# Two layer entries of a hybrid decoder step: zero products at the start, weights and squares queued elsewhere

## The chip, the core and the metric

The kernel runs on one core of a Trainium2 chip. The engines are named as in the profile: PE (TensorE; PEld is its weight load), DVE (VectorE), ACT (ScalarE), POOL (GpSimd) and SP (SyncE, which here only issues DMAs). Each takes its instructions in the order in which they were laid out. The metric is the device time of one execution in microseconds; a kernel's time is the median of its runs.

## The reference, cut to what matters

One inference step of two layers over 1024 prompt tokens and 8 x 8 sample tokens, 1088 rows of 1024 in all. Layer 0 is a Mamba-2 SSD mixer, layer 1 latent attention (MLA). The change touches how each layer begins:

```python
ln_p = rms_norm(hp, norm_w[i]); ln_s = rms_norm(hs, norm_w[i])
# layer 0
proj = jnp.einsum('btd,de->bte', h, w_in)           # 1024 -> 2048 + 4096 + 32
xbc, new_buf = causal_conv(xbc, conv_buf, conv_w, conv_b)   # needs the last 3 rows of state_conv
# layer 1
proj = jnp.einsum('btd,de->bte', h, w_in)           # 512 + 256 + 32 + 1024 (gate)
```

`rms_norm` divides each row by the root of its mean square and multiplies with a weight per column. Everything is float32.

## The kernel before, in words

Each operand of a large product is held as two float32r parts, high and low: `split` (L123) casts on ACT and subtracts on DVE or POOL. A product is then three matmuls, high-high, high-low, low-high (`proj_piece`, L84 inside `mm3`).

The rows are handled as nine tiles (`TILES`: eight of 128, one of 64) in three token groups (`TG`: 384, 384, 320). `norm_steps` is the entry of both layers. For each group, `norm_cols` takes eight column steps `d`: three transposes on PE into a PSUM tile `xtp` (L244), the high part on ACT with the norm weight as scale (L246, tile `xh` in the first layer, `hh` in the second; the instructions are kept in `k.cols`), and the low part on DVE (L247, `xl`, `hl`). Between column steps, `steps` runs one piece of projection per group and block.

First entry (`norm_rows`): rows are loaded by SP (L704, L706; `XB` buffers), squared on ACT with a running sum (L227), and the inverse root is taken by DVE (L198) and POOL's power (L203), for the first group row by row, for the other two once a group; DVE scales the row (L234). The squares of the next group are queued on ACT behind column step `SQ + j` of the group before. The function `before` loads the small vectors and the weights of projection blocks 0 and 1, each in two parts (`WPARTS`, L281, cast L125, low part L126). The function `after` runs behind the first group: `ssd_consts` (small constants, `alog`, masks) and `conv_state_T`, which loads 96 state rows (`cst`, L316) and transposes them on PE (`cvp`, L321). Block 2's weights are cast behind the eighth column of the first group; their DMAs are not held. Their low parts and those of the gate weights `zd` (`load_zdt`, L337 to L341) are made on POOL. Blocks 0 and 1 are projected together, group by group, then blocks 2 and 3, then the gates (`pz`, L96).

Second entry (`tail=True`): the rows `xrb` come out of the last projection of the SSD layer (`ssd_out`; DVE adds L804, L806), are stored to `h_d`, squared on ACT into a spare tile `tok` (L814), and scaled by `scale_row` (L209). The rows 6 to 8 are scaled ahead of the first column step. Two gate blocks (`gate_block`: weights `wgh`, `wgl`, the low part on POOL) are projected together meanwhile; the evacuation of their pieces is a SiLU on ACT (L921).

Who goes first on an engine is decided by a planner that lays all instructions out on a modelled clock. `issue_after(ins)` adds an edge: what is traced inside it on the engine of `ins` is laid out behind `ins`, without a wait for its end. `keep_in_program_order` puts one instruction behind everything traced before it on its engine.

Of the kernel before, what the change touches and what calls it, by code (L numbers as in the profile page):

```python
# [16 lines left out]
D = 1024  # L17
# [41 lines left out]
XDB = 2  # L59
SQ = 2  # L60
YB = 2
SCAN = "csccsccsccscc"
XB = 6
WPARTS = 2
# [57 lines left out]

def split(k, hi, lo, src, eng=None):  # L123
    nc = k.nc
    nc.scalar.copy(hi, src)  # L125
    (eng or nc.vector).tensor_tensor(lo, src, hi.bitcast(F32), op=ALU.subtract)  # L126
# [69 lines left out]
def rstd_of(k, out, ssq, n):  # L196
    nc = k.nc
    nc.vector.tensor_scalar(out, ssq, 1.0 / n, EPS, op0=ALU.mult, op1=ALU.add)  # L198
    m, n = out.shape[0], int(np.prod(out.shape[1:]))
    e = k.nhalf[:m, :n]  # L200
    if len(out.shape) == 3:
        e = e.rearrange("p (a b) -> p a b", a=out.shape[1])
    nc.gpsimd.tensor_tensor(out, out, e, op=ALU.pow)  # L203

# [8 lines left out]
def norm_rows(k, gi, load, pool, xbufs):  # L213
# [7 lines left out]
    for j, i in enumerate(idx):  # L221
# [3 lines left out]
        sq = k.sqp(f"sq{i}")  # L225
        with k.tc.issue_after(k.cols[gi - 1][SQ + j].ins) if gi else nullcontext():
            nc.scalar.activation(sq[:m], xt[:m], AF.Square, accum_out=ssq[:m, j : j + 1])  # L227
# [10 lines left out]
def norm_cols(k, gi, xs, wcol, hi, lo, psum):  # L238
    nc = k.nc
    t0, n = TG[gi]  # L240
    for d in range(8):
        p = psum.tile([128, 512], F32, tag="tr", name=f"xtp{gi}_{d}", bufs=PB["tr"])
        for xt, m, o in xs:
            nc.tensor.transpose(p[:, o : o + m], xt[:m, d * 128 : d * 128 + 128], k.ident[:m, :m])  # L244
        k.cols[gi].append(
            nc.scalar.activation(hi[:, d, t0 : t0 + n], p[:, :n], AF.Copy, scale=wcol[:, d : d + 1]))  # L246
        nc.vector.scalar_tensor_tensor(  # L247
            lo[:, d, t0 : t0 + n], p[:, :n], wcol[:, d : d + 1], hi[:, d, t0 : t0 + n].bitcast(F32),
            op0=ALU.mult, op1=ALU.subtract)
    if gi == 2:  # L250
# [3 lines left out]
def norm_steps(k, load, wcol, hi, lo, pool, psum, steps, xbufs, before=None, after=None, tail=False):  # L254
    if tail:
        for i in range(6, 9):
            k.hrows.append(scale_row(k, i, pool))
    rows = k.hrows[:3] if tail else norm_rows(k, 0, load, pool, xbufs)
    if before is not None:
        before()  # L260
        wcol = k.normc[0]
    k.cols = [[], [], []]
# [15 lines left out]

def load_w(k, pool, src, nk, ncol, tag, bufs=3, raws=None, rbufs=2, eng=None):
# [4 lines left out]
    split(k, hi, lo, raw, eng)  # L284
    return hi, lo


def load_parts(k, pool, src, nk, parts, tag, bufs, raws=None, rbufs=2, eng=None):
    n = nk // parts
    return [x for j in range(parts)  # L290
            for x in kslices(load_w(k, pool, src[128 * n * j : 128 * n * j + 128 * n], n, src.shape[1], tag, bufs,
                                    raws, rbufs, eng), n)]

# [124 lines left out]
class Group:  # L418
# [28 lines left out]

    def weights(self, bi):
        k, g = self.k, self.g
        col = (DIN + DIN + 128 * g, DIN + DIN + 1024 + 128 * g, DIN + 256 * g, DIN + 256 * g + 128)[bi]  # L450
        return load_parts(k, self.wp, k.I["ssd_w_in"][0][:, col : col + 128], 8, WPARTS, "wi", WB, self.raws.get(bi), RB,
                          k.nc.gpsimd if g == 0 and bi > 1 else None)
# [246 lines left out]
def x_loader(k):  # L699
    I = k.I  # L700

    def load(xt, i):
        if i < 8:
            k.nc.sync.dma_start(xt, I["x_prompt"][0, i * 128 : i * 128 + 128])  # L704
        else:
            k.nc.sync.dma_start(xt[:64], I["x_sample"].rearrange("b t d -> (b t) d"))  # L706

# [81 lines left out]
def ssd_out(k, items, ypools, psum):  # L789
# [3 lines left out]
    for n, (ph, i) in enumerate(items):  # L793
# [3 lines left out]
        for hf in range(2):  # L797
# [13 lines left out]
        (nc.gpsimd if ph.k0 and i > 6 else nc.sync).dma_start(k.h_d[t0 : t0 + m], xr[:m])  # L811
        if ph.k0:
            sq = k.tok.rearrange("p i a h -> p (i a h)")[:, :D]
            nc.scalar.activation(sq[:m], xr[:m], AF.Square, accum_out=k.hssq[:m, i : i + 1])  # L814
            rstd_of(k, k.hrs[:m, i : i + 1], k.hssq[:m, i : i + 1], D)
            k.hr.append((xr, m))
            if i < 6:
                k.hrows.append(scale_row(k, i, k.h0p))
# [3 lines left out]
def layer_ssd(k):  # L822
# [8 lines left out]
    with ExitStack() as st:  # L831
# [14 lines left out]
        with open_pool(tc, name="x0", bufs=1, side="right") as p0:  # L846
# [15 lines left out]
        for _ in range(6):  # L862
            next(st0)
# [52 lines left out]
def gate_block(k, wp, raws, b):  # L916
    ws = kslices(load_w(k, wp, k.I["mla_w_in"][0][:, 800 + 128 * b : 928 + 128 * b], 8, 128, "wg", 3, raws, eng=k.nc.gpsimd), 8)
    gt = wp.tile([128, T], F32, tag="gt", name=f"gt{b}", bufs=2)
# [1073 lines left out]
```

## Time and profile before

| | |
|---|---|
| median of three runs | 1969.62 us |
| runs | 1965.58, 1969.62, 1971.59 us |
| profiled execution, its own time | 1968.92 us |
| its span in the profile | 1967.1 us |
| mean granted clock of PE | 0.992 |
| DMA over the span | 202.00 MB, mean 103 GB/s |

The span runs from the first to the last instruction of the profiled execution; the time of an execution has a little more around it. A row of the timeline reads: start, duration (of all that is merged in the row), engine, line, operation, output tile, input tiles, shapes, count, and in brackets how long the engine had idled and what ended it. `x2` behind a row means that two instructions are merged into it. Matmul durations overlap, so their starts give the rate. In the waits, the numbers are the total in us, the count and the longest.

### The profile page before, as it was taken

The page shows a single profiled execution, that of the slowest core. Times are in us where ns is not written, and L with a number is a line of the kernel's source. Part 1 is how long each engine was busy: PE and PEld are TensorE (multiplying, and loading weights), DVE is VectorE, ACT ScalarE, POOL GpSimd, SP SyncE. Part 2 cuts the span into 40 slices and gives each one's busy share as a digit, 9 for nine tenths or more (in the row PEclk, how much of TensorE's full clock was granted, in tenths as well). Part 3 has the DMA queues.
Part 4 walks back from the last instruction along what each step waited for, and adds up shares of the span by engine and source line. Part 5 has one row for each costly group of instructions (what it writes and reads, how often), then busy time and mean ns, then how long its engine had stood idle before and what let it go on. Part 6 is the DMA issues. An engine that isn't in the chain of part 4 may idle for free. (4 is left out here: it accounts for less than half of the span.)

```text
span 1967.1 us, 33409 instructions
## 1 busy us (share of the span) xinstructions
PE 1902.0 (97%) x12001; PEld 1732.5 (88%) x12001; DVE 1188.6 (60%) x2407; ACT 1109.2 (56%) x2535; POOL 822.2 (42%) x1017
## 2 busy tenths in 40 slices
PE   6999999999999999899999999999999999899998
PEld 5999999999999999788787998898888888688887
DVE  4547566666665666765533104466787887666674
ACT  5456666666666676742214314335777776755552
POOL 1537555555655555444003212103343434745441
PEclk9999999999999999999999999999999999999999
DMA  5223333333333332554534333132121113554441
GB/s 153 59 59 89 95 85 94 85 103 88 92 86 94 78 101 68 194 169 148 183 116 116 121 146 95 56 107 76 46 68 40 51 42 86 180 188 143 143 126 38
DMA packets 181085, 202.00 MB, mean 103 GB/s; under 512 B 18828, under 2 KB 147608, under 8 KB 180536
## 3 DMA queue, kind: packets, MB, share of 16 engines
q1 hardware_dynamic: 175864, 180.08, 30.1%
q0 software_dynamic: 4976, 19.66, 3.0%
q8 instruction: 95, 1.56, 0.3%
q14 instruction: 70, 0.57, 0.1%
q10 hardware_dynamic: 80, 0.13, 0.0%
HBM read 146.52 MB, written 53.28 MB: 102 GB/s over the span
## 5 line engine op out<-in xcount | busy, mean ns | idle before, releaser
L84 PE MATMUL pj<-xh,wih 128*128 128x384 f32 (+1 forms) x768 | 255.3, 336 | 4.4 <-ACT xh L246 3.9
L84 PE MATMUL pj<-xl,wih 128*128 128x384 f32 (+1 forms) x768 | 254.8, 332 | 0.6 <-DVE xl L247 0.6
L84 PE MATMUL pj<-xh,wil 128*128 128x384 f32 (+1 forms) x768 | 254.1, 331 | 0.0
L1354 POOL TENSOR_TENSOR tl<-P,th 128x384 fp32r<-128x384 f32 (+1 forms) x96 | 90.7, 945 | 238.5 <-ACT P L1352 192.7
L483 DVE SCALAR_TENSOR_TENSOR acc<-raw,vec,acc 128x1112 f32<-128x1112 f32 x96 | 142.1, 1481 | 25.7 <-ACT acc L479 24.7
L84 PEld LDWEIGHTS pj<-xh,wih 128*128 128x128 f32 x768 | 144.6, 189 | 6.3 <-ACT xh L246 4.5
L84 PEld LDWEIGHTS pj<-xl,wih 128*128 128x128 f32 x768 | 145.1, 189 | 1.9 <-DVE xl L247 0.9
L84 PEld LDWEIGHTS pj<-xh,wil 128*128 128x128 f32 x768 | 145.0, 189 | 0.4
L96 PE MATMUL pz<-wih,xh 128*128 128x256 f32 x504 | 142.8, 287 | 1.1 <-ACT z L524 1.1
L96 PE MATMUL pz<-wil,xh 128*128 128x256 f32 (+1 forms) x504 | 140.2, 284 | 0.0
L1351 ACT ACTIVATE th<-st 128x512 fp32r<-128x512 f32 x192 | 94.4, 492 | 73.0 <-PE st L1347 52.6
L587 ACT ACTIVATE M<-M,tok 128x128 f32<-128x128 f32 (+1 forms) x288 | 90.9, 386 | 68.2 <-DVE M L584 67.9
L96 PE MATMUL pz<-wih,xl 128*128 128x256 f32 x448 | 128.3, 286 | 0.0
L1639 POOL TENSOR_TENSOR kvl<-pgr,kvh 128x512 fp32r<-128x512 f32 x64 | 85.3, 1350 | 74.3 <-ACT kvh L1637 74.3
L96 PEld LDWEIGHTS pz<-wih,xh 128*128 128x128 f32 x504 | 95.9, 190 | 1.9 <-ACT z L524 1.6
L584 DVE TENSOR_TENSOR M<-M,negu 128x512 f32<-128x512 f32 x64 | 52.2, 816 | 69.8 <-DMA M<-acs_d 69.6
L1352 ACT ACTIVATE P<-st 128x512 f32<-128x512 f32 x192 | 93.5, 487 | 0.0
L96 PEld LDWEIGHTS pz<-wil,xh 128*128 128x128 f32 (+1 forms) x504 | 92.7, 184 | 0.7
L126 DVE TENSOR_TENSOR wil<-wraw,wih 128x512 fp32r<-128x512 f32 x88 | 70.5, 807 | 29.5 <-ACT wih L125 26.6
L96 PEld LDWEIGHTS pz<-wih,xl 128*128 128x128 f32 x448 | 85.3, 190 | 0.1
L570 POOL TENSOR_TENSOR xdd<-xsT,tok 128x256 f32<-128x256 f32 x64 | 50.8, 794 | 80.4 <-ACT xsT L556 80.0
L1354 DVE TENSOR_TENSOR tl<-P,th 128x512 fp32r<-128x512 f32 x96 | 69.2, 721 | 21.9 <-ACT P L1352 21.5
(826 smaller groups left out, 6296.3 us busy)
## 6 DMA issues: line engine op xcount, KB each, us to landing
wraw<-in_ssd_w_in SPq DMA_DIRECT2D x92, 256.0 KB
M<-acs_d SPq DMA_DIRECT2D x64, 256.0 KB
s<-in_state_ssm SPq DMA_DIRECT2D x32, 256.0 KB
y_d<-y SPq DMA_DIRECT2D x64, 128.0 KB
out_s_ssm<-s SPq DMA_DIRECT2D x32, 256.0 KB
wraw<-in_ssd_w_out SPq DMA_DIRECT2D x12, 512.0 KB
q_d<-qt SPq DMA_DIRECT2D x32, 192.0 KB
qp<-q_d SPq DMA_DIRECT2D x8, 768.0 KB
```

What stands on the lines that cost most here:

```text
L84: nc.tensor.matmul(out, a, b, start=(i == 0), stop=(i == n - 1))
L96: nc.tensor.matmul(o, a, b, start=(j == 0), stop=(j == len(ops) - 1))
L126: (eng or nc.vector).tensor_tensor(lo, src, hi.bitcast(F32), op=ALU.subtract)
L483: last = nc.vector.scalar_tensor_tensor(acc, raw[:, j : j + n], k.convw[j][:, blk : blk + 1], acc, op0=ALU.mult, op1=ALU.add)
L570: nc.gpsimd.tensor_tensor(v3(xdd), v3(xsT), hb(2), op=ALU.mult)
L584: nc.vector.tensor_tensor(M[:m, :, :m], M[:m, :, :m], (k.negs if smp else k.negu)[:m, :m].unsqueeze(1).to_broadcast([m, 4, m]), op=ALU.add)
L587: nc.scalar.activation(M[:m, h, :m], M[:m, h, :m], AF.Exp, bias=tk[:, 0, 4 * g + h : 4 * g + h + 1])
L1351: nc.scalar.activation(th[:, :n], ps[:, :n], AF.Exp, scale=SCALE)
L1352: nc.scalar.activation(P[:, :n], ps[:, :n], AF.Exp, scale=SCALE)
L1354: eng.tensor_tensor(tl[:, :n], P[:, :n], th[:, :n].bitcast(F32), op=ALU.subtract)
L1639: nc.gpsimd.tensor_tensor(rl[:, j : j + 2], raw[:, j : j + 2], rh[:, j : j + 2].bitcast(F32), op=ALU.subtract)
```

## The change

1. An activation table is loaded at the start of ACT's queue.
2. Eight products of a zeroed tile (128x128 by 128x256, plain float32) are put at the start, two more behind the second and one behind the third transpose of column step 1 of the first group. Nothing reads their output.
3. The cast and subtraction of the second part of block 1's weights are queued behind the third column step (`late`).
4. In the first entry each row gets its own inverse root, the squares of the next group come one column step later, and there is one row buffer more.
5. `conv_state_T` runs behind the second group; `ssd_consts` is traced behind the whole entry, its exponential and masks held behind late instructions of the entry.
6. Block 2's weights are loaded behind the last x row on SP and cast behind the eighth column of the second group.
7. In the second entry the last row is squared behind the third column step, the last three rows are scaled behind low columns 4 to 6 (counted from 0), and the store of the last row is issued behind the first group.
8. The low part of the gate weights is made in four instructions instead of one.

```diff
-SQ = 2
+WARM = (8, 2, 1)
+SQ = (3, 3)
-XB = 6
+XB = 7
@@ split: parts > 0 subtracts in that many slices
+    for a in range(parts):
+        s = slice(a * n, a * n + n)
+        (eng or nc.vector).tensor_tensor(lo[:, s], src[:, s], hi[:, s].bitcast(F32), op=ALU.subtract)
@@ setup
+    tc.keep_in_program_order(nc.scalar.preload_act_table_set("exp_and_others"))
@@ ssd_consts
-    nc.scalar.activation(k.alog, k.alog, AF.Exp)
+    with k.tc.issue_after(k.cols[1][7].ins):
+        nc.scalar.activation(k.alog, k.alog, AF.Exp)
...
-        nc.gpsimd.tensor_scalar(neg, mask, -NEG, NEG, op0=ALU.mult, op1=ALU.add)
+        with k.tc.issue_after(k.pow.ins):
+            nc.gpsimd.tensor_scalar(neg, mask, -NEG, NEG, op0=ALU.mult, op1=ALU.add)
@@ new
+def warm_open(k, pool, psum):
+    k.wsrc = pool.tile([128, 256], F32, name="wsrc")
+    k.nc.gpsimd.memset(k.wsrc, 0.0)
+    k.wout = psum.tile([128, 512], F32, tag="pj", name="wout", bufs=PB["pj"])
+
+def warm(k, n):
+    for _ in range(n):
+        k.nc.tensor.matmul(k.wout[:, :256], k.wsrc[:, :128], k.wsrc, start=True, stop=True)
+
+def square_row(k, i, junk):
+    xr, m = k.hr[i]
+    k.nc.scalar.activation(junk[:m], xr[:m], AF.Square, accum_out=k.hssq[:m, i : i + 1])
+    rstd_of(k, k.hrs[:m, i : i + 1], k.hssq[:m, i : i + 1], D)
@@ norm_rows
-        with k.tc.issue_after(k.cols[gi - 1][SQ + j].ins) if gi else nullcontext():
+        with k.tc.issue_after(k.cols[gi - 1][SQ[gi - 1] + j].ins) if gi else nullcontext():
...
-        if gi == 0:
-            rstd_of(k, rs[:, j : j + 1], ssq[:, j : j + 1], D)
-    if gi:
-        rstd_of(k, rs, ssq, D)
+        k.pow = rstd_of(k, rs[:, j : j + 1], ssq[:, j : j + 1], D)
@@ norm_cols
+            if k.late and d == 1 and j:
+                with k.tc.issue_after(tr.ins):
+                    warm(k, WARM[j])
...
+        if d == 2 and k.late:
+            with k.tc.issue_after(k.cols[gi][-1].ins), k.tc.issue_after(k.lows[-1].ins):
+                split(k, *k.late.pop())
@@ norm_steps
-    if tail:
-        for i in range(6, 9):
-            k.hrows.append(scale_row(k, i, pool))
...
+        if tail and gi == 0:
+            with k.tc.issue_after(k.cols[0][2].ins), k.tc.issue_after(k.lows[2].ins):
+                square_row(k, 8, pool.tile([128, D], F32, tag="sq", name="hsq8", bufs=1))
+            for i in range(6, 9):
+                with k.tc.issue_after(k.lows[i - 2].ins):
+                    k.hrows.append(scale_row(k, i, pool))
...
-        if after is not None and gi == 0:
+        if after is not None and gi == 1:
             after()
...
+        if tail and gi == 0:
+            xr, m = k.hr[8]
+            k.tc.keep_in_program_order(k.nc.gpsimd.dma_start(k.h_d[TILES[8][0] : T], xr[:m]))
@@ Group.block
-        with k.tc.issue_after(k.cols[0][7].ins) if first else nullcontext():
+        with ExitStack() as es:
+            if first:
+                es.enter_context(k.tc.issue_after(k.cols[1][7].ins))
+                es.enter_context(k.tc.issue_after(k.xl_dma.ins))
             ws = self.pre.pop(bi, None) or self.weights(bi)
@@ layer_ssd
+            warm_open(k, p0, psum)
+            warm(k, WARM[0])
...
-                for bi in range(2):
-                    g0.pre[bi] = g0.weights(bi)
+                g0.pre[0] = g0.weights(0)
+                k.late = []
+                g0.pre[1] = g0.weights(1, k.late)
...
             def after():
-                ssd_consts(k)
                 conv_state_T(k, p0, psum)
...
+        ssd_consts(k)
@@ gate_block
-raws, eng=k.nc.gpsimd), 8)
+raws, eng=k.nc.gpsimd, sub=4), 8)
```

In `ssd_out` the square of the last row and its store are left to `norm_steps`; `k.xl_dma` is the load of the last x row.

More of the change, by code (lines that the diff above doesn't have):

```diff
@@ L120, with split @@
     pass
-def split(k, hi, lo, src, eng=None):
+def split(k, hi, lo, src, eng=None, parts=0):
     nc = k.nc
     nc.scalar.copy(hi, src)
-    (eng or nc.vector).tensor_tensor(lo, src, hi.bitcast(F32), op=ALU.subtract)
+    n = parts and hi.shape[1] // parts
+    for a in range(parts):
+        s = slice(a * n, a * n + n)
+        (eng or nc.vector).tensor_tensor(lo[:, s], src[:, s], hi[:, s].bitcast(F32), op=ALU.subtract)
+    if not parts:
+        (eng or nc.vector).tensor_tensor(lo, src, hi.bitcast(F32), op=ALU.subtract)
 def setup(k, stack):
@@ L202, in rstd_of @@
         e = e.rearrange("p (a b) -> p a b", a=out.shape[1])
-    nc.gpsimd.tensor_tensor(out, out, e, op=ALU.pow)
+    return nc.gpsimd.tensor_tensor(out, out, e, op=ALU.pow)
+def square_row(k, i, junk):
+    xr, m = k.hr[i]
+    k.nc.scalar.activation(junk[:m], xr[:m], AF.Square, accum_out=k.hssq[:m, i : i + 1])
+    rstd_of(k, k.hrs[:m, i : i + 1], k.hssq[:m, i : i + 1], D)
 def scale_row(k, i, pool):
@@ L276, in load_raw, with load_w @@
     return t.rearrange("p (k e) -> p k e", k=nk)
-def load_w(k, pool, src, nk, ncol, tag, bufs=3, raws=None, rbufs=2, eng=None):
+def load_w(k, pool, src, nk, ncol, tag, bufs=3, raws=None, rbufs=2, eng=None, sub=0, late=None):
     raw = load_raw(raws or pool, nk, ncol, rbufs)
@@ L283, in load_w, with load_parts @@
     lo = pool.tile([128, nk, ncol], F32R, tag=tag + "l", name=tag + "l", bufs=bufs)
-    split(k, hi, lo, raw, eng)
+    if late is None:
+        split(k, hi, lo, raw, eng, sub)
+    else:
+        late.append((hi, lo, raw))
     return hi, lo
-def load_parts(k, pool, src, nk, parts, tag, bufs, raws=None, rbufs=2, eng=None):
+def load_parts(k, pool, src, nk, parts, tag, bufs, raws=None, rbufs=2, eng=None, late=None):
     n = nk // parts
@@ L291, in load_parts @@
             for x in kslices(load_w(k, pool, src[128 * n * j : 128 * n * j + 128 * n], n, src.shape[1], tag, bufs,
-                                    raws, rbufs, eng), n)]
+                                    raws, rbufs, eng, late=late if j == parts - 1 else None), n)]
 def kslices(w, n):
@@ L446, in pair, with weights @@
             self.conv_out()
-    def weights(self, bi):
+    def weights(self, bi, late=None):
         k, g = self.k, self.g
@@ L451, in weights @@
         return load_parts(k, self.wp, k.I["ssd_w_in"][0][:, col : col + 128], 8, WPARTS, "wi", WB, self.raws.get(bi), RB,
-                          k.nc.gpsimd if g == 0 and bi > 1 else None)
+                          k.nc.gpsimd if g == 0 and bi > 1 else None, late)
     def block(self, bi, acc):
@@ L705, in load @@
         else:
-            k.nc.sync.dma_start(xt[:64], I["x_sample"].rearrange("b t d -> (b t) d"))
+            k.xl_dma = k.nc.sync.dma_start(xt[:64], I["x_sample"].rearrange("b t d -> (b t) d"))
     return load
@@ L810, in ssd_out @@
                 yield
-        (nc.gpsimd if ph.k0 and i > 6 else nc.sync).dma_start(k.h_d[t0 : t0 + m], xr[:m])
+        if i < 8 or not ph.k0:
+            (nc.gpsimd if ph.k0 and i > 6 else nc.sync).dma_start(k.h_d[t0 : t0 + m], xr[:m])
         if ph.k0:
-            sq = k.tok.rearrange("p i a h -> p (i a h)")[:, :D]
-            nc.scalar.activation(sq[:m], xr[:m], AF.Square, accum_out=k.hssq[:m, i : i + 1])
-            rstd_of(k, k.hrs[:m, i : i + 1], k.hssq[:m, i : i + 1], D)
             k.hr.append((xr, m))
+            if i < 8:
+                square_row(k, i, k.tok.rearrange("p i a h -> p (i a h)")[:, :D])
             if i < 6:
@@ L916, in gate_block @@
 def gate_block(k, wp, raws, b):
[L917 removed]
+    ws = kslices(load_w(k, wp, k.I["mla_w_in"][0][:, 800 + 128 * b : 928 + 128 * b], 8, 128, "wg", 3, raws, eng=k.nc.gpsimd, sub=4), 8)
     gt = wp.tile([128, T], F32, tag="gt", name=f"gt{b}", bufs=2)
```

11 lines of the change are left out of this document (6 added, 5 removed).

## The prediction

> **What bounds the kernel now.** The page comes first: TensorE (PE) is busy for almost the whole span, so only time in which PE stands, or runs slowly, can be won.
>
> ```profile
> span 1967.1 us, 33409 instructions
> PE 1902.0 (97%) x12001; PEld 1732.5 (88%) x12001; DVE 1188.6 (60%) x2407; ACT 1109.2 (56%) x2535; POOL 822.2 (42%) x1017
> ```
>
> Then the table of waits, for PE alone, in the two stretches that the change touches: 0 to 140 us (entry of the SSD layer), and in a second fence 1030 to 1130 us (entry of the MLA layer).
>
> ```profile
> PE vecp L186 <- DMA r<-in_ssd_conv_w: 8.3, 1, 8.3
> PE pj L84 <- ACT xh L246: 3.9, 2, 3.5
> PE cvp L321 <- DMA cst<-in_state_conv: 2.2, 1, 2.2
> ```
>
> ```profile
> PE pj L84 <- ACT hh L246: 3.7, 1, 3.7
> ```
>
> Three waits of 2 to 4 us, besides the first data. Then the stretches themselves (columns: length, busy time of PE with its instructions, granted clock, DMA share, GB/s; the last row has all five engines between length and clock):
>
> ```profile
> 15.50:19.20 3.70, 3.66 (x14) 1.00 0.37 118
> 29.20:33.50 4.30, 3.98 (x18) 0.60 0.60 121
> 1059.80:1063.40 3.60, 3.58 (x13) 0.54 0.33 92
> 60.00:70.00 10.00, 10.00 (x64) 9.92 (x63) 9.89 (x7) 4.22 (x7) 9.08 (x7) 1.00 0.19 53
> ```
>
> Behind the second and third wait the granted clock is 0.60 and 0.54. The first stretch says 1.00, but its products show otherwise; the timeline has them 0.32 us apart early and 0.18 us apart later, with the same shape:
>
> ```profile
> 17.65 0.52 PE L84 MATMUL pj<-xh,wih 128*128 128x384 f32 x1
> 17.97 0.52 PE L84 MATMUL pj<-xl,wih 128*128 128x384 f32 x1
> ...
> 23.80 0.35 PE L84 MATMUL pj<-xl,wih 128*128 128x384 f32 x1
> 23.98 0.34 PE L84 MATMUL pj<-xh,wil 128*128 128x384 f32 x1
> ```
>
> So each stop is paid twice: the wait, then about 4 us at half rate. The row of 60 to 70 us shows PE without a gap once the first entry is over: what is won before it should reach the end.
>
> **First entry: the first product.** The timeline of ACT and PE:
>
> ```profile
> 4.01 1.28 ACT L227 ACT_TABLE_LOAD   x1 [4.01 <-DMA xt<-in_x_prompt]
> 7.73 1.06 ACT L227 ACTIVATE sq<-xt 128x1024 f32<-128x1024 f32 x1 [0.24 <-DMA xt<-in_x_prompt]
> 11.33 0.69 PE L244 MATMUL xtp<-ident,xt 128*128 128x128 f32 x2 [0.58 <-DVE xt L234]
> 11.63 0.62 ACT L125 CAST wih<-wraw 128x512 fp32r<-128x512 f32 x1 [0.26 <-DMA wraw<-in_ssd_w_in]
> 14.38 0.62 ACT L125 CAST wih<-wraw 128x512 fp32r<-128x512 f32 x1 [2.14 <-DMA wraw<-in_ssd_w_in]
> 14.91 1.05 ACT L246 ACTIVATE xh<-xtp,vec 128x384 fp32r<-128x384 f32 x2
> 15.54 1.01 PE L84 MATMUL pj<-xh,wih 128*128 128x384 f32 x2 [3.52 <-ACT xh L246]
> ```
>
> The transposes are there at 11.33, but ACT, which works in order, stands in front of the fourth weight cast, whose data comes at 14.38. The change puts that cast behind the third column (`late`). ACT is then free after the third cast, 11.63 + 0.62 = 12.25; a column takes half of 1.05, so the first product starts near 12.9 instead of 15.54: **2.6 us**. By then two more columns are done, at about 14.3, and the cast meets its data. Ends: 3.3 us if the planner puts the column before the third cast as well, 1.0 us if the new products hold the transposes up (below). The preloaded table takes 1.28 us off the first two squares, not off the third, which waited for its own row at 7.73: nothing, and if that row came sooner, the casts would still hold. The seventh row buffer moves one load forward into a queue that has room (18 to 21 us below): nothing.
>
> **The unread products.** 128x128 by 128x256 in plain f32; the decay sums are the same shape, each issued as two rows:
>
> ```profile
> 117.38 0.70 PE L367 MATMUL dpa<-dta,masku 128*128 128x256 f32 x2 [0.51 <-DVE dta L361]
> 118.01 0.41 PE L368 MATMUL dpa<-dta,masks 64*128 64x32 f32 x2
> ```
>
> One costs 118.01 - 117.38 = 0.63 us, at half rate 1.26. Eight take 5.0 to 10.1 us from about 1 us on, ending at 6 to 11 us. PE has nothing else before 8.3 us (its first wait above); at the worst end the first transposes are some 3 us late, which eats most of the gain above, hence its end of 1.0. The three others, 1.9 us, fall among the transposes before 12.9, where PE had waited 3.52 us. What they buy: 3.7 us at 0.32 instead of 0.18 us a product, 3.7 x 0.14 / 0.32 = **1.6 us**; ends 0 and 1.6, and I take 1.6, since the two later stretches show a clock that opens after about 4 us of work.
>
> **The state rows.** Their load, their transposes, and the DMA queue just before (second fence, all engines, a DMA share of 0.04):
>
> ```profile
> 20.22 1.64 SPq L316 DMA_DIRECT2D cst<-in_state_conv  x4
> 28.28 0.52 PE L321 MATMUL cvp<-ident,cst 96*128 96x96 f32 x4 [2.23 <-DMA cst<-in_state_conv]
> ```
>
> ```profile
> 18.00:21.00 3.00, 3.00 (x18) 2.87 (x17) 1.10 (x2) 2.49 (x6) 0.59 (x2) 1.00 0.04 7
> ```
>
> PE reaches the transposes 2.23 us before the rows land, 8 us after issue; block 2's weights and the last x rows were queued around them. Behind it lie 4.3 us at 0.60. The change asks for the rows after the second group's columns are laid out, and queues block 2's weights behind the last x row and their casts behind the eighth column of that group; those weights are needed only when block 2 starts. The saving is 2.23 + 4.3 x 0.4 = 3.9 us. But the same eight transposes return inside the third group, behind a new load that waits for a square's buffer. If PE meets it as early as now, nothing is saved. I take a quarter of the wait as kept: **2.9 us**, ends 0 and 3.9.
>
> What feeds the second group: its squares start one column later, but each row now gets its own root. A product group takes 1.39 us of PE a column step (next fence), 11.1 us for eight; ACT needs for eight columns and three squares about 8 x 0.55 + 3 x 1.25 = 8.2 us (column and square from the rows above, 0.19 more for the sum), plus the late cast. It fits.
>
> ```profile
> 22.77 0.51 PE L84 MATMUL pj<-xh,wih 128*128 128x384 f32 x2
> 24.16 0.52 PE L84 MATMUL pj<-xh,wih 128*128 128x384 f32 x2
> ```
>
> First entry: 2.6 + 1.6 + 2.9 = 7.1 us.
>
> **Second entry.**
>
> ```profile
> 1050.71 4.75 POOL L126 TENSOR_TENSOR wgl<-wraw,wgh 128x1024 fp32r<-128x1024 f32 x2 [0.18 <-ACT wgh L125]
> 1054.94 1.14 PE L244 MATMUL xtp<-ident,xt 128*128 128x128 f32 x9
> 1055.14 0.68 DVE L804 TENSOR_TENSOR xrb<-xrb,pob 64x512 f32<-64x512 f32 x1 [2.27 <-PE pob L96]
> 1055.75 1.40 DVE L209 TENSOR_SCALAR xt<-xrb,hrs 128x1024 f32<-128x1024 f32 x2
> 1057.18 0.69 DVE L806 TENSOR_TENSOR xrb<-xrb,pob 64x512 f32<-64x512 f32 x1
> 1057.95 1.06 ACT L814 ACTIVATE tok<-xrb 64x1024 f32<-64x1024 f32 x1 [4.80 <-issue]
> 1059.18 1.52 ACT L246 ACTIVATE hh<-xtp,vec 128x384 fp32r<-128x384 f32 x3
> 1059.82 0.82 PE L84 MATMUL pj<-hh,wgh 128*128 128x384 f32 x2 [3.73 <-ACT hh L246]
> ```
>
> Nine transposes are done by 1056.1, yet ACT first squares the last row, which DVE finishes only after scaling two rows that nobody needs until the third group. The change queues this square behind the third column and the scalings behind the fifth to seventh low column. The first three transposes are ready near 1055.3; a column of 0.55 us, and the first product starts at 1055.9: 3.9 us sooner. With no long stop, 3.6 us at 0.54 go too, 1.7 us. Against it, DVE still has its two adds (0.68 + 0.69, to 1056.5) before the first low column at about 1057.1, and PE has only 0.3 us of other work there: 0.9 us is given back. **4.7 us**; ends 3.0 (the clock falls all the same) and 5.6 (the low column comes first). Square and scalings move under the 11.1 us of the first group. Splitting the POOL subtraction in four keeps its sum: the first pair of 4.75 us ends at 1055.5 in either form, before 1055.9; if four cost more, the second gate block pays tenths. The store of the last row goes behind POOL's splits; the rows are read back only by the last projection.
>
> **The sum.** 7.1 + 4.7 = 11.8. The profiled execution took 1968.92 us, 0.7 below the median 1969.62 of runs from 1965.58 to 1971.59: 1968.92 - 11.8 = **1957.1 us**.
>
> **Rivals.** (1) *POOL does not come along.* The gate weights of group 0 are split on POOL just in time:
>
> ```profile
> 75.50 6.79 POOL L341 TENSOR_TENSOR zdl<-wraw,zdh 128x288 fp32r<-128x288 f32 x4
> 81.88 0.38 PE L96 MATMUL pz<-zdh,xh 128*128 128x288 f32 x1
> ```
>
> The last part is ready at 82.3, and PE needs it some 3 us after 81.88. If POOL kept its clock time, 7.1 - 2.9 = 4.2 us would be lost: 1961.3. Against: its first split waits for transposes and casts that PE itself releases. (2) *The clock shuts again* between the eight products and the first real one, since only transposes and three products lie there: the 1.6 us stay, 1958.7. For: a dozen transposes before 15.54 did not open it. [...] No run so far has products among transposes. [...] (3) *The state rows' wait only moves* into the third group: the 2.9 us stay, 1960.0. For: the planner put these transposes 2.23 us too early once. (4) *Slower.* One planner lays out all engines on its own clock, and every ready time after 12 us shifts. The tightest place is the scan of the groups, where the state product already waits for POOL (waits of PE, 140 to 1030 us):
>
> ```profile
> PE st L84 <- POOL xddl L126: 3.6, 2, 2.5
> ```
>
> If a new order put that product ahead of POOL's split in each of the seven groups after the first, 7 x 2.5 = 17.5 us would be lost: 1974.6. It wins from five such waits on (12.5 against 11.8). For: it happens twice now. Against: all that it needs is released by PE, which shifts as a whole. That the change does not do what it says is unlikely, as the orders it writes are fixed edges on the engine named.
>
> **How the numbers follow.** Forecast 0.48, (1) 0.10, (2) 0.12, (3) 0.14, (4) 0.16. A difference of 0.3%, 5.9 us, is about what a measurement of this kernel can tell from none. Faster by more means under 1963.7: nearly all of the forecast and most of (1) to (3), 0.77; within, the weak ends of these and a quarter of (4), 0.11; slower 0.12, the rest of (4). Range: both best ends give 8.9 + 5.6 = 14.5 us, 1954.4, less 4 us of scatter between runs, 1950; (1) and (3) together 1964.2, with 2 us of scatter 1966.
>
> **What would show it.** The first product near 12.9 us, 0.18 us apart from the start; no PE wait on the state rows; the third group's last product about 7 us sooner; the first gate product near 1056 with a granted clock of 1.00. Wrong if the first eight products end after 10 us, if a wait of 2 us stands before the state transposes, or if PE's waits between 140 and 1030 us grow.

## The result, and the profile after

| | before | changed |
|---|---|---|
| median of runs taken side by side, us | 1970.73 (12 runs) | 1965.11 (12 runs) |
| ratio, with its 95% interval | | 0.9972 [0.9959, 0.9985] |
| profiled execution, us | 1968.92 | 1965.69 |
| its span, us | 1967.1 | 1963.9 |

The change gained 0.28%, 5.6 us (1970.73 x 0.0028), where 11.8 us were forecast. The page of the changed kernel has the same picture of the engines, with 22 more TensorE products and 22 more weight loads: the eleven unread products, two rows each.

```profile
span 1963.9 us, 33491 instructions
PE 1907.8 (97%) x12023; PEld 1737.6 (88%) x12023; DVE 1192.2 (61%) x2411; ACT 1109.3 (56%) x2535; POOL 828.8 (42%) x1046
```

The table of waits of PE from 0 to 140 us, against 8.3, 3.9 and 2.2 us before:

```profile
PE wout L190 <- POOL ssq L245: 1.2, 1, 1.2
PE xtp L267 <- DVE xt L257: 0.9, 2, 0.5
PE pj L85 <- ACT xh L272: 0.6, 1, 0.6
```

Of the 3.5 us in front of the first product 0.55 us are left, and the 2.2 us in front of the state transposes are gone. The timeline of PE and ACT in the same stretch:

```profile
1.16 6.30 PE L190 MATMUL wout<-wsrc 128*128 128x256 f32 x16 [1.16 <-POOL ssq L245]
11.15 0.62 ACT L126 CAST wih<-wraw 128x512 fp32r<-128x512 f32 x1 [0.19 <-DMA wraw<-in_ssd_w_in]
12.31 0.62 PE L85 MATMUL pj<-xh,wih 128*128 128x384 f32 x2 [0.55 <-ACT xh L272]
13.64 0.33 PE L85 MATMUL pj<-xh,wil 128*128 128x384 f32 x1
13.81 0.34 PE L85 MATMUL pj<-xh,wih 128*128 128x384 f32 x1
14.14 0.61 ACT L126 CAST wih<-wraw 128x512 fp32r<-128x512 f32 x1
```

Eight unread products end at 7.46 us, the first real one starts at 12.31 us, products follow each other by 0.17 us (13.64, 13.81) instead of 0.32, and the fourth cast finds its data there. The two stretches that were at half rate or stopped before, and the start of the second entry (columns as in the prediction, all five engines):

```profile
15.50:19.20 3.70, 3.70 (x26) 3.59 (x25) 2.62 (x6) 3.70 (x8) 1.09 (x2) 1.00 0.51 177
29.20:33.50 4.30, 4.30 (x31) 4.19 (x30) 3.98 (x10) 3.61 (x9) 2.16 (x5) 1.00 0.26 85
1046.00:1050.00 4.00, 3.04 (x20) 2.49 (x21) 2.34 (x4) 2.54 (x6) 2.61 (x4) 1.00 0.83 231
```

26 products against 14 in the first, 31 against 18 in the second, both at 1.00 (the first said 1.00 before as well; there the spacing of the products tells the two apart). At the second entry the clock stays open too, but PE has a wait that it had not (waits of PE, 1030 to 1130 us, and the timeline of the place):

```profile
PE xtp L267 <- DVE xrb L848: 1.6, 1, 1.6
```

```profile
1046.82 1.17 PE L267 MATMUL xtp<-ident,xt 128*128 128x128 f32 x9 [1.59 <-DVE xrb L848]
1048.09 0.61 PE L85 MATMUL pj<-hh,wgh 128*128 128x384 f32 x2
```

How far the changed kernel is ahead can be followed through the program: for each kind of VectorE, ScalarE and GpSimd instruction that both traces hold in the same number, the n-th start of the one is set against the n-th of the other, and the median is taken in stretches of 40 us. This lead over the trace of before is 9.5 us after the first entry, 9.9 us ahead of the second and 13.0 us behind it (1120 to 1280 us): in this pair of traces the forecast's sum was there, and somewhat more. (One pair says little on the size: with the second trace of each kernel, runs 5 and 7 below, the four pairs give 5.6 to 19.0 us there, 12.3 in the mean.) At the end it is 3.2 us. From 1280 to 1440 us it falls by 4.0 to 9.0, and **from 1440 to 1600 us by 8.9 to 0.1**. There ACT, which works in order, stands twice in front of a cast; these are the timeline's rows of the load, the cast and the next score product of PE:

```profile
1449.08 0.39 SPq L1243 DMA_DIRECT2D w<-in_mla_w_uk  x1
1454.06 0.62 ACT L126 CAST w<-w 128x512 fp32r<-128x512 f32 x1 [2.64 <-DMA w<-in_mla_w_uk]
1455.20 0.50 PE L1386 MATMUL st<-qTh,kTh 98*128 98x512 f32 x1 [1.94 <-ACT P L1398]
...
1539.97 0.39 SPq L1243 DMA_DIRECT2D w<-in_mla_w_uk  x1
1545.13 0.62 ACT L126 CAST w<-w 128x512 fp32r<-128x512 f32 x1 [2.86 <-DMA w<-in_mla_w_uk]
1546.27 0.80 PE L1386 MATMUL st<-qTh,kTh 98*128 98x512 f32 x1 [2.18 <-ACT P L1398]
```

The same loads and casts before:

```profile
1458.10 0.40 SPq L1197 DMA_DIRECT2D w<-in_mla_w_uk  x1
1460.78 0.62 ACT L125 CAST w<-w 128x512 fp32r<-128x512 f32 x1 [0.34 <-DMA w<-in_mla_w_uk]
1545.11 0.39 SPq L1197 DMA_DIRECT2D w<-in_mla_w_uk  x1
1547.78 0.62 ACT L125 CAST w<-w 128x512 fp32r<-128x512 f32 x1 [0.38 <-DMA w<-in_mla_w_uk]
```

A load of 256 KB takes 2.7 us from issue to cast before and 5.0 and 5.2 us after. The exponentials behind the cast come late, PE stops for about 2 us, and both stops are followed by a stretch at half clock (windows of the changed kernel):

```profile
1457.10:1460.50 3.40, 3.40 (x10) 2.67 (x9) 2.78 (x6) 3.01 (x6) 1.46 (x2) 0.50 0.00 0
1545.80:1552.60 6.80, 6.33 (x19) 5.23 (x20) 4.19 (x9) 5.42 (x12) 1.74 (x2) 0.50 0.00 0
```

Nothing of this is in the code that the change touches. What differs is what the DMA queues do while the load is under way. The view of DMA, from the load's issue to its cast, changed kernel first, then the kernel before (packets, MB, share of 16 engines):

```profile
q1 hardware_dynamic: 372, 0.43, 28.5%
q8 instruction: 1, 0.02, 1.6%
q14 instruction: 1, 0.01, 0.4%
```

```profile
q1 hardware_dynamic: 276, 0.27, 29.4%
```

In the changed kernel a packet of the instruction queue q8 falls into the load. Two other things in this window are not the cause. The smaller packet of q14 falls into the first of the two loads alone, 3.3 us behind its issue, and not into the second, which is as late; in run 3 below it meets neither. And the transfers that the core itself queues around the loads (gate rows, a store) stand at the same distance behind each load in all traces, within 0.1 us; the first fence has more packets because its window is longer. The page counts the q8 packets (number, MB, share):

```profile
q8 instruction: 95, 1.56, 0.3%
```

95 packets of 16 KB for 2 x 12023 rows of products and weight loads are one for every 253; with the semaphore rows of TensorE's queue counted too, they are 255.5 rows apart in the mean (256.4 before), and when the n-th packet starts (n from 0), 256 n rows and 152 to 227 more have started, for all 95. In time they are 13 to 32 us apart, so they follow the count of TensorE instructions, not the time. The one at 1450.50 us came when 18612 rows of TensorE's queue had started, semaphore rows included, and so did the one at 1463.01 us before; but with 44 more at the start the same count is reached 44 instructions earlier in the code. It took 1.29 us, where a packet of 1 KB of the load takes 0.046 us (median of its 256). Between the first and the last packet of the load lie 1.26 us before and 2.85 us after.

None of TensorE's waits in the trace is put down to such a packet. The load beside it took 5.0 us instead of 2.7.

### The profile page after: what moved, and what is told of

Read it like the earlier page. It is cut to its first block, busy times and chain, and to the rows that moved or that the text cites. A ratio compares the mean times of both kernels' runs of the same rounds, so it can differ in the third digit from the quotient of the medians.

```text
span 1963.9 us, 33491 instructions
## 1 busy us (share of the span) xinstructions
PE 1907.8 (97%) x12023; PEld 1737.6 (88%) x12023; DVE 1192.2 (61%) x2411; ACT 1109.3 (56%) x2535; POOL 828.8 (42%) x1046
## 4 chain that ended last, share of the span: by engine, by line
PE 77%; DVE 7%; ACT 6%; DMA 6%; POOL 2%; issue 2%; SPq 0%; ACTq 0%; POOLq 0%; DVEq 0%
PE pj L85 19%; PE pz L97 8%; PE pq L97 5%; PE pob L97 5%; PE poa L97 5%; PE p L97 4%; PE py L634 2%; DMA M<-acs_d 2%; PE o L85 2%; PE sc L85 2%; PE st L1386 2%; PE sc L1354 2%; PE o L1417 1%; PE st L1387 1%; PE st L1388 1%
```

## The experiments

**Fetch theory**: the 44 instructions of the unread products move the packets of the instruction queue onto two loads, and that costs most of what is missing, in every run. **Chance theory**: stops and half-clock stretches in the heads fall where they like; the count of instructions is of no account. Times stand beside the kernel before on the same chip, which ran 1970.7 to 1972.6 us in its medians, so ratios are compared.

*1. No products, the late block kept.*

```diff
-WARM = (8, 2, 1)
+WARM = (0, 0, 0)
...
-            warm_open(k, p0, psum)
```

> The changed kernel without the eleven unread products (and without their zero tile); the late block split and everything else stay. Two theories of where the forecast's gain went. Fetch theory: the eleven products are 44 TensorE instructions more (22 products and 22 weight loads, since each fp32 product is two passes), and the packets of 16384 bytes of the instruction queue, which come every 256 TensorE instructions, fall 44 instructions earlier in the code; two of them then fall on two loads of w from w_uk, ScalarE stands 2.6 and 2.9 us on them, and the clock falls twice behind it. Without the products the packets stand again where they stood before: w loads of about 2.7 us, no ScalarE wait over 0.6 us on them, no half clock at about 1455 and 1546 us; the 9 us lost between 1285 and 1550 us come back, the 3 us that the changed kernel had regained by 1720 us are given back, and the start pays 1.6 to 2 us for the clock: 1960.5 us, between 1957 and 1963. Chance theory: the half-clock stretches in the attention fall where they like in each run; the number of TensorE instructions is of no account; only the start pays: 1966.7 us, between 1965 and 1969.

Measured: 1963.39 us, ratio 0.9951 [0.9936, 0.9967], beside 0.9972 with the products. Its two casts:

```profile
1454.26 0.62 ACT L126 CAST w<-w 128x512 fp32r<-128x512 f32 x1 [0.35 <-DMA w<-in_mla_w_uk]
1541.69 0.62 ACT L126 CAST w<-w 128x512 fp32r<-128x512 f32 x1 [0.41 <-DMA w<-in_mla_w_uk]
```

No packet meets the loads, neither cast waits long, and there is no half clock behind them. From 1440 to 1600 us it loses 0.9 us instead of 8.9. It is faster than the changed kernel by the medians, though the intervals overlap, and although it starts worse: its products from 12.52 to 17.8 us are mostly 0.32 us apart, and its lead after the first entry is 7.2 us instead of 9.5. As a ratio it has won 9.7 us, within the expectation of the fetch theory; its time, beside a kernel before of 1972.41 us, lies just outside.

*2. The same products in twice as many instructions.*

```diff
-WARM = (8, 2, 1)
+WARM = (16, 4, 2)
...
-        k.nc.tensor.matmul(k.wout[:, :256], k.wsrc[:, :128], k.wsrc, start=True, stop=True)
+        k.nc.tensor.matmul(k.wout[:, :128], k.wsrc[:, :128], k.wsrc[:, :128], start=True, stop=True)
```

> The changed kernel with each unread product cut in two of half the width (22 products of 128x128 for 11 of 128x256): the same TensorE time at the start within 0.5 us, the same order on every engine, and 44 TensorE instructions more. Fetch theory: the packets of the instruction queue fall 44 instructions (about 4 us) earlier again, ahead of the issue of the two w loads: these loads take about 2.7 us, the two ScalarE waits of 2.6 and 2.9 us and the half clock behind them go, 5 to 9 us: 1958 us, between 1955 and 1961, unless the packets meet another load, which the trace would show as another wait on a DMA. Chance theory: 1965 us, between 1963 and 1967.

Measured: 1963.29 us, ratio 0.9961 [0.9945, 0.9976].

```profile
1453.01 0.62 ACT L126 CAST w<-w 128x512 fp32r<-128x512 f32 x1 [0.37 <-DMA w<-in_mla_w_uk]
1540.17 0.62 ACT L126 CAST w<-w 128x512 fp32r<-128x512 f32 x1 [0.41 <-DMA w<-in_mla_w_uk]
```

Both stalls go, as the fetch theory has it, though the products are there and the order of all other instructions on PE, ACT, DVE and POOL is the same in the two traces: it is the count that decides, not the products. The size was overstated: 0.0011 to the changed kernel is 2 us, not 5 to 9, and the interval does not tell it from none. The time alone lies where the chance theory put it (1963 to 1967); it is the waits that speak against that theory.

*3. The kernel before with the products alone* (the first eight ahead of everything, two and one in the second column's transposes).

```diff
+WARM = (8, 2, 1)
...
+            if k.late and d == 1 and j:
+                with k.tc.issue_after(tr.ins):
+                    warm(k, WARM[j])
...
+        k.late = gi == 0 and not tail
...
+            warm_open(k, p0, psum)
+            warm(k, WARM[0])
```

> The kernel before with nothing but the eleven unread products (eight ahead of all, two and one between the transposes of the second column). Fetch theory: the same 44 TensorE instructions more as in the changed kernel, so both w loads take about 5 us and ScalarE stands on them for over 2 us, with half clock behind; 9 us lost in the attention, some 3 regained behind it, 1.6 won at the start: 1975 us, between 1972 and 1979, slower than before. Chance theory: only the start's 1.6 us: 1969 us, between 1967 and 1971.

Measured: 1978.05 us, ratio 1.0025 [1.0010, 1.0040]: slower, by 4.9 us. Both stalls have come with the products:

```profile
1463.66 0.62 ACT L126 CAST w<-w 128x512 fp32r<-128x512 f32 x1 [2.65 <-DMA w<-in_mla_w_uk]
1554.68 0.62 ACT L126 CAST w<-w 128x512 fp32r<-128x512 f32 x1 [2.79 <-DMA w<-in_mla_w_uk]
```

Here the products win nothing at the start (the lead after the first entry is -0.1 us): the first real product starts at 15.38 us, PE stands four times between the unread products and it, 0.6 to 1.4 us each, and the clock is at half again from 12.4 us, with products 0.32 us apart at 17.17, 17.49 and 17.81 us.

*4. The loads of w a group of heads earlier, with a second buffer.*

```diff
+        self.w8b = vp.tile([128, 2, 256], F32, name="w8b")
...
+    def load_group(self, hg):
+        cs = slice(256 * hg, 256 * hg + 256)
+        for t, w in (((self.w8[0], self.w8b)[hg % 2], self.wuk), (self.w8[1], self.wuv)):
+            self.k.nc.sync.dma_start(t, w[:, cs].rearrange("(k p) e -> p k e", p=128))
...
+            if i == 5 and hg < MH // 4 - 1:
+                self.load_group(hg + 1)
```

> The changed kernel with w_uk and w_uv of the next four heads loaded one group of heads ahead, w_uk into a second buffer; the TensorE instruction count stays. Fetch theory: the packets stay where they are, but nothing waits any more for the loads that they meet; the two ScalarE waits and the half clock behind them go, 5.5 to 7 us; the loss of 1.9 us at 1285 us stays: 1959 us, between 1956 and 1962. Chance theory: half clock comes in other places in its stead: 1965 us, between 1963 and 1967.

Measured: 1961.83 us, ratio 0.9943 [0.9929, 0.9957]: just inside the range expected (1956 to 1962), but by half of the way only, so the number is in part luck:

```profile
1451.88 0.39 SPq L1241 DMA_DIRECT2D w8b<-in_mla_w_uk  x1
...
1457.05 0.62 ACT L126 CAST w<-w8b 128x512 fp32r<-128x512 f32 x1 [2.84 <-DMA w8b<-in_mla_w_uk]
```

The planner moved the cast forward with the load. So the load for the last group stands where that of the third stood, meets the packet there, and ACT waits again; only the stall near 1545 us is gone. The lead lost from 1440 to 1600 us is 4.2 us, for one stall instead of two.

*5. The changed kernel again.*

> The changed kernel once more, nothing edited: what of its trace comes again. Fetch theory: both w loads of about 5 us and the ScalarE waits of 2.6 and 2.9 us on them come again, within 0.1 us, with half clock within 5 us behind each; ratio 0.9972 within its interval of 0.0013. Chance theory: the waits and the half clock stand elsewhere.

Measured: 1967.59 us beside 1972.34, ratio 0.9974 [0.9964, 0.9984]. Both waits on the casts come again, the second 1 us shorter than expected:

```profile
1459.17 0.62 ACT L126 CAST w<-w 128x512 fp32r<-128x512 f32 x1 [2.63 <-DMA w<-in_mla_w_uk]
1549.27 0.62 ACT L126 CAST w<-w 128x512 fp32r<-128x512 f32 x1 [1.91 <-DMA w<-in_mla_w_uk]
```

Half clock follows the first, at 1461.7 us; behind the second, where PE itself stops for 1.23 us only, there is none. The stalls are systematic, the half clock behind them is not quite. From 1440 to 1600 us 5.6 us are lost.

*6. The cast held back.* The load stays, but its cast is laid out behind the last exponential ahead of it in the program, 28 ACT instructions later; the order on PE is unchanged.

```diff
+        self.last = nc.scalar.activation(P[:, :n], ps[:, :n], AF.Exp, scale=SCALE)
...
-        split(k, *self.wk, self.wkr)
+        with k.tc.issue_after(self.last.ins) if hg else nullcontext():
+            split(k, *self.wk, self.wkr)
```

> The changed kernel with the cast of w (and its rest) held behind the last exponential that stands ahead of it in the program, about 28 ScalarE instructions later; the loads, the TensorE order and its count stay. Fetch theory: the two loads still take about 5 us, but nobody stands on them; the two stalls and the half clock behind them go, 5.5 to 7 us against the changed kernel run beside it: a ratio of 0.9940 to before (0.9930 to 0.9950), 11 to 12 us, which is what was forecast. Chance theory: a ratio of 0.9972, as for the changed kernel.

Measured: 1962.06 us, ratio 0.9936 [0.9920, 0.9952] beside the 0.9974 of run 5: **12.6 us faster than before**, with an interval that does not touch the changed kernel's. It beats both kernels. (The held casts were not tried in the kernel before. In the traces they win nothing over it there: from 1440 to 1600 us the four kernels with held casts lose 0.1 to 0.7 us against the trace of before.)

```profile
1470.87 0.62 ACT L126 CAST w<-w 128x512 fp32r<-128x512 f32 x1
1558.29 0.62 ACT L126 CAST w<-w 128x512 fp32r<-128x512 f32 x1
```

No wait in front of either. The packets still fall 1.03 and 1.04 us behind the loads' issue; nothing stands on the loads any more. From 1440 to 1600 us 0.4 us are lost.

*7. The kernel before again.*

> The kernel before once more, for a second trace: how far two executions of one program part. If the stretch from 120 to 840 us is a matter of chance, this trace is 2 to 5 us longer there than the one that the forecast was made from, as the traces of three of the variants have been; if those lost their lead there by their earlier start, it is within 1 us. The w loads take 2.7 us in both theories.

Measured: 1975.38 us in one run; by 840 us its trace is 6.7 us behind the first trace of the same program, 6.2 us of it lost from 120 us on, and it is 5.8 us or more behind from there to the end. So that stretch parts two executions of one program by more than was expected, and the trace that the forecast was made from was a lucky one there; leads at the end of single traces mean little, losses at one place repeated over many traces mean much.

*8. The second entry as before.*

```diff
+    if tail:
+        for i in range(6, 9):
+            k.hrows.append(scale_row(k, i, pool))
...
-            with k.tc.issue_after(k.cols[0][2].ins), k.tc.issue_after(k.lows[2].ins):
-                square_row(k, 8, pool.tile([128, D], F32, tag="sq", name="hsq8", bufs=1))
...
-            if i < 8:
+            if i < 9:
                 square_row(k, i, k.tok.rearrange("p i a h -> p (i a h)")[:, :D])
```

> The changed kernel with the second entry as it was (the last square, the last three rows and their store ahead of the columns again); the first entry's changes stay, and so does the TensorE count. The forecast priced the second entry at 4.7 us; the traces show between 1.9 us and 4.6 us of lead won there. Both theories: 2 to 5 us slower than the changed kernel run beside it, a ratio of 0.9982 to 0.9997 to before; the waits on the w loads come again by the fetch theory.

Measured: 1970.64 us, ratio 0.9989 [0.9978, 0.9999]. Against run 5 the second entry's part is worth 0.0015, 3.0 us, where 4.7 were forecast, but the two intervals overlap and do not tell 3.0 from 4.7. Nor is this quite the entry of before: `wout` is still there, and the nine transposes wait 2.91 us for the last add, which they did not before. Both waits on w come again (2.70 and 1.99 us).

*9 and 10. An unused tile ahead of the products' output*, with the casts held (9) and without (10). `wout` is the first PSUM tile asked for, with tag `pj`; without products the first is of tag `tr`.

```diff
+    psum.tile([128, 512], F32, tag="tr", name="wtr", bufs=PB["tr"])
     k.wout = psum.tile([128, 512], F32, tag="pj", name="wout", bufs=PB["pj"])
```

> The changed kernel with the casts of w held as above, and ahead of the products' output tile one unused tile of the tag tr. The output tile (tag pj) is the first that the first PSUM pool hands out in the changed kernel; so pj takes the banks that tr had, and in the next pool the first transposes (tag tr) take a bank from which VectorE still reads pob: they wait 1.6 us for it at the second entry in every trace with the products and the second entry's change, and in the one without the products they do not. With the unused tile first, the banks are as before. Bank theory: no wait of the transposes on xrb at the second entry; the lead won there rises from 2.6 to 3.1 us to some 4.6 us, as without the products: a ratio of 0.9928, between 0.9915 and 0.9940. Rival (the wait hides work that must come anyway, the last low column): the transposes go earlier, the first gate product waits instead, and the ratio stays 0.9936.

> The changed kernel with the unused tile of the tag tr alone; the casts of w stand as in the changed kernel. Bank theory: 1.6 to 2 us less than the changed kernel, a ratio of 0.9965 against 0.9974, the two waits on the w loads as there. Rival: 0.9974.

Measured: 0.9954 [0.9940, 0.9968] and 0.9972 [0.9959, 0.9986]. The transposes of the first column no longer wait, but those of the second do (run 9):

```profile
1049.21 0.49 PE L268 MATMUL xtp<-ident,xt 128*128 128x128 f32 x3
1050.96 0.85 PE L268 MATMUL xtp<-ident,xt 128*128 128x128 f32 x6 [1.26 <-DVE xrb L849]
1051.56 0.60 PE L85 MATMUL pj<-hh,wgh 128*128 128x384 f32 x2
```

The lead won at the second entry rises from 3.1 us to 4.2 and 4.0 us, towards the 4.6 expected, but the ratios do not show it: run 9 lies outside its range (0.9915 to 0.9940) and is no faster than run 6. 1 us is less than these runs can tell.

*11. Both edits, and the products halved as in run 2.*

> The kernel with both edits (held casts, unused tile) and each product cut in two (44 TensorE instructions more). If the held casts make the heads indifferent to where the packets of the instruction queue fall, the ratio is that of the kernel with both edits run beside it within 0.0015; if other loads are met and waited for, it is over 0.0015 slower and the trace shows a TensorE wait on a DMA that the other lacks.

Measured: 0.9944 [0.9926, 0.9962] against 0.9954 in run 9. Within 0.0015: with the casts held, it no longer matters where the packets fall, as far as these runs can tell.

*12. Three unused tiles* (`tr`, `tr`, `pj`), casts held, so that both rings should stand as without products.

> The changed kernel with the casts of w held and three unused tiles ahead of the products' output tile (tr, tr, pj), so that both rings, tr and pj, stand at every later tile as they did without products. With one unused tile the wait on the last add went from the first column of transposes to the second (1.3 us). Ring theory: no transpose waits for xrb at the second entry, the first gate product starts about 1.75 us after the last product of the projection, as without the products (2.9 us in the changed kernel, 2.4 us with one unused tile), and the lead won there is 4.6 us: a ratio of 0.9930, between 0.9915 and 0.9945. Rival (one us of PE there does not reach the end measurably): the trace as said, the ratio as with the casts alone, 0.9936 to 0.9954.

Measured: 1960.97 us, ratio 0.9939 [0.9920, 0.9957]. The wait stays on the second column, 1.26 us, so my account of the rings is at best half right. That the tile `wout` brought the wait of the first column is shown (run 1, without it, has no wait on the last add there and wins 4.6 us of lead; runs 9 to 12 have the wait moved); that it does so through the PSUM bank that the transposes get is my reading, which no trace shows, and what holds the second column stays open.

The traces of runs whose loads stand where they did, in one table. Packet: how long after the issue of the load of w a packet of the instruction queue starts (us, third and fourth group of heads; the nearest one). Lost: the lead lost from 1440 to 1600 us against the first trace of before.

```
kernel            TensorE extra   packet after issue   lost   ratio
before again            0            5.7    4.0         0.5    -
1 no products           0            5.5    4.4         0.9   0.9951
changed                44            1.4    2.4         8.9   0.9972
5 changed again        44            1.0    1.0         5.6   0.9974
8 entry one alone      44            1.3    1.1         5.2   0.9989
10 unused tile         44            1.1    2.4         9.3   0.9972
3 products alone       44            1.1    2.0         6.6   1.0025
2 halves               88           -0.3   -4.2         0.6   0.9961
6 casts held           44            1.0    1.0         0.4   0.9936
9 held, tile           44            1.3    1.0         0.7   0.9954
11 held, halves        88           -0.9   -4.2         0.3   0.9944
12 held, three tiles   44            1.1    2.3         0.1   0.9939
```

Where a packet starts 1.0 to 2.4 us behind the issue and ACT stands on the load, 5.2 to 9.3 us are lost; where either is missing, 0.1 to 0.9 us. (Run 4, with its loads at other places, had one such meeting and lost 4.2 us.)

## Why the prediction was wrong

*What bounds the kernel*: right, with one sentence that was wrong and decides the case, the step that failed: **"what is won before it should reach the end"**. The lead was 13.0 us at 1280 us (12.3 in the mean of four pairs of traces), more than the 11.8 of the sum, and 8.9 us of it went at two loads; 5.2 to 9.3 us went there in every trace in which packets met both and ACT stood on them. I had read PE's row of 60 to 70 us as a proof that a stretch without gaps passes a lead on. In this pair of traces it did between the entries (9.5 us behind the first, 9.9 ahead of the second), but the packets of the instruction queue came by the count of TensorE instructions (255.5 rows apart in the mean) instead of by the time, and the 44 new instructions shifted exactly that. I had priced the products in PE time alone (0.63 us each), and asked only what they hold up: the price of their 44 instructions for the loads behind was put at nothing.

*First product*: forecast near 12.9 us, measured 12.31, with products 0.17 us apart from 13.64 us; inside the ends given. *The unread products*: they ended at 7.46 us, within 6 to 11, and held nothing up. Forecast 1.6 us for the clock. Run 1, without them, is 2.3 us less far ahead after the first entry than the changed kernel, and 1.7 us less than run 5; in run 3, where the first real product was late, they won nothing. *The state rows*: a quarter of the 3.9 us was taken as kept (the text says "of the wait", the sum takes it of both); all of it went, at a clock of 1.00. Together the first entry won 9.5 us (8.9 in run 5) on the traces where 7.1 were forecast. It erred to the low side.

*Second entry*: the clock stays open, as forecast (1.00 from 1046 to 1050 us; in run 2 it does not: half clock from 1051.5 us), but the sum of 4.7 us was too high: 3.1 us on the trace, as in run 5. A second, smaller step that failed: I let the first transposes be "ready near 1055.3" without a wait. They wait 1.59 us for the last add once the new output tile is in the kernel; an edit of the first entry was priced there alone. Without that tile, in run 1, the second entry wins 4.6 us: the 4.7 were right for the entry by itself.

*The rivals*: none came. The gate weights of group 0 came along, the clock did not shut ahead of the first product (0.17 us from one to the next at 13.64 us), no wait stands on the state rows, and the scan kept its order: PE's waits between 140 and 1030 us did not grow (those over 0.1 us sum to 17.3 us before and 16.8 after). The slower case had the right kind of thought, a place far behind the entries that answers to a shift, but looked for it in the order of instructions, and the order had not changed.

*The sum*: the mechanism was right at both entries, and with the two loads out of the way the same change gives 12.6 us (run 6), 12.0 (run 12), 9.1 (run 9) and 11.0 (run 11), around the 11.8 forecast. The range held the result, but by luck: its slow end stood for rivals (1) and (3), and neither came. The outcome that was given 0.77, faster by more than 0.3%, did not come either; 0.28% belongs to the one that was given 0.11.

What stays open: what holds the second column in runs 9 to 12, and two losses between 1280 and 1440 us: 1.9 to 2.5 us near 1285 us, which three traces show (changed, 8, 12) and others with the same count do not, and 1.1 to 1.5 us near 1350 us in six traces (changed, 4, 5, 6, 9, 12), whose half clock there lasts 6.83 us instead of 3.41.

## What to carry to other kernels

When an edit adds or removes instructions on an engine, ask not only what they take but what they shift: here the packets of the instruction queue came one for 255.5 rows of TensorE's queue, and 44 more rows put two of them onto loads that ACT, which works in order, waited for with no slack (2.64 and 2.86 us instead of 0.34 and 0.38). A wait that is met "just in time" (0.3 to 0.4 us here) is the place to look; a cast that is needed some 30 us later (cast at 1454.06 us in the changed kernel, the first product on it at 1486.0 us) should not stand directly behind its load. And a new tile, whose content nothing reads, can still bring a wait elsewhere: with `wout` the transposes of the second entry stood 1.59 us for the last add, without it (run 1) they did not.

## What the hardware did that was not expected

- Where a packet of the instruction queue (16 KB) met a load of w, the load of 256 KB took 4.2 to 5.3 us from issue to cast instead of 2.7 us (changed kernel and runs 3, 4, 5, 8 and 10). The delay, 1.5 to 2.6 us, is longer than the packet, which took 1.29 and 0.95 us in the changed kernel. There 240 of the load's 256 packets start up to 2.32 us behind its issue; before, all 256 start up to 2.28 us behind it. The last 16 start from 2.70 us on, and in the second load from 3.30 us, where the instruction packet ends (2.71 and 3.31 us), and the last of them ends 1.2 and 1.3 us behind that; why these 16 start so late was not tried by itself.
- Stops of PE of 1.94 and 2.18 us were followed by 3.41 and 6.83 us at half clock, and the one of 2.23 us at the first entry before the change by 3.41 us; a stop of 1.23 us (run 5, second load) was not, and neither was one of 2.1 us (run 3, second load). The half-clock stretches that lie whole inside the span are 3.41 us long (ten) or 6.83 us (four) in the traces of before and of the changed kernel.
- Two executions of the unchanged kernel were 6.7 us apart by 840 us, and in both the longest single wait of PE in that stretch is 2.5 us.
